# Two-layer hybrid encoder on one core: when the next layer's key and value weights are loaded, which engine copies the gates, and when gathered tokens are turned

## The chip, the cores and the metric

The kernel runs on one core of a Trainium2 chip. Its time is the device time of that core in microseconds (us), as the median of several executions. All arithmetic is in fp32 or in pairs of split values that together stand for fp32.

## The reference

A trunk of two layers on 512 tokens of 1024 features. Each layer has a mixing block, a cross-attention into 256 memory tokens, and 16 experts of which each picks its own 64 tokens. The change touches the third block and, inside it, the keys and values of the next layer's cross-attention.

```python
# cross-attention (one per layer): keys and values depend on mem and on weights alone
kv = (mem_n @ w_kv).reshape(b, m, 2, X_HEADS, X_HEAD_DIM)
...
# experts
logits = jnp.einsum('bsd,de->bse', h, w_router, preferred_element_type=jnp.float32)
aff = jax.nn.softmax(logits, axis=-1)
gates, idx = lax.top_k(aff.transpose(0, 2, 1), cap)
xs = h[b_ix, idx]
a = jnp.einsum('becd,edf->becf', xs, w_gate)
u = jnp.einsum('becd,edf->becf', xs, w_up)
y = jnp.einsum('becf,efd->becd', jax.nn.silu(a) * u, w_down)
y = y * gates[..., None].astype(y.dtype)
return jnp.zeros_like(h).at[b_ix, idx].add(y)
```

## The kernel before

**Pairs and steps.** The expert stage of a layer goes through eight pairs of experts (`pr` 0 to 7). A pair has 64 + 64 = 128 gathered tokens, one expert in each half of TensorE's columns. Its products come in eight chunks, after each of which `between(i)` runs what the tables `todo` and `plan` hold for that step: steps 0 to 3 follow four chunks of the gate and up products (32 matmuls of `xT`, two weight loads each), steps 4 to 7 four chunks of the down products (16 matmuls of `hT`, one load each). A pair therefore has twelve weight loads of 2 MB, which SyncE issues in order (`wload`, L1081).

**Weight buffers.** A load takes the next buffer of the list `order`, in rotation: seven of a ring ("w"), one in `kvp` ("k") and one in `pair` ("x"). A load waits until TensorE has read what stood in its buffer, and all later loads stand behind it in SyncE's queue. While the next layer's keys and values are computed, `kv_start` takes "k" and two of the ring out of the list, which leaves six; two come back after the last product.

**The tokens of the next pair** are found by VectorE and TensorE in steps 0 to 2, and fetched at step 3 (pair 0: step 4): GpSimd writes an iota, VectorE makes the indices, GpSimd starts an indirect transfer into the tile `xr` (`gather`, L1217). Each row of it carries 1024 features and the token's gates. `scalars` then copies three narrow columns (`rsl`, a token's scale, and `gx`, the gate of either expert) on GpSimd, behind the transfer. `next_turned` at steps 5 and 6 (pair 0: 6 and 7) turns the tokens into `xT` with 4 + 4 transposes on TensorE (L1203).

**What uses them.** ScalarE's `hs` (L1320) scales by `rsl`; `yhl` (L164 and L165, the split of a down result) scales by `gx`. `yhl` goes to TensorE, which scatters it back to the 512 tokens (L1339, L1340).

**Next layer's keys and values** are computed inside the expert stage of layer 0, at steps counted over all pairs (step 22 is pair 2, step 6). `kv_start` loads `mem` at 22 and takes the buffers, `mem_scaled` follows at 23, four `mem_turned` at 24 to 27 (L366 on TensorE). Then, eight times: `kv_load` brings 1 MB of weights at 28 + 4u, two `kv_split` at 29 + 4u and 30 + 4u make split copies of it on ScalarE and VectorE (L161, L162, tile `wkv`), `kv_products` at 31 + 4u multiplies. `mem` and all eight loads go through one buffer (tag "e") and GpSimd's queue, the queue of the gathers too (L1240). The place of an instruction in an engine's row is settled by a scheduler, which may move a transfer ahead of code written before it.

Of the kernel before, what the change touches and what calls it, by code (L numbers as in the profile page):

```python
# [29 lines left out]
D = 1024  # L30
# [5 lines left out]
NE = 16  # L36
# [55 lines left out]
def build(tc, a, out, packed):  # L92
    nc = tc.nc
# [4 lines left out]
    def pool(stack, name, bufs=1, **kw):  # L98
        return stack.enter_context(tc.tile_pool(name=name, bufs=bufs, reuse_waits="tile", **kw))
# [3 lines left out]
    pair = pool(es, "pair")  # L103
    RD, RM = 3, 7
    kvp = pool(es, "kvp", side="right")
    KV_STEP = 22
    ring, ex_ = [None], [None]
    order = deque()
    halves = []
# [10 lines left out]
    def bank2():  # L120
        turn[0] ^= 1
        return bank("ms"[turn[0]])
# [25 lines left out]
    def load(src, b, c):  # L148
        t = room(b, c)
        nc.sync.dma_start(t, src)  # L150
        return t
# [7 lines left out]
    def split_ps(p, hi, lo, col=None):  # L159
        if col is None:  # L160
            first = nc.scalar.activation(hi, p, AF.Copy)  # L161
            nc.vector.tensor_tensor(lo, p, hi.bitcast(F32), op=ALU.subtract)  # L162
        else:
            first = nc.scalar.activation(hi, p, AF.Copy, scale=col)  # L164
            nc.vector.scalar_tensor_tensor(lo, p, col, hi.bitcast(F32), op0=ALU.mult, op1=ALU.subtract)  # L165
        latest[0] = first
        return first
# [52 lines left out]
    def tsl(t):  # L220
        return slice(t * P, (t + 1) * P)

    def nosync(after, before, why):
        tc.add_manual_dep(after.ins, before.ins.name,
                          mybir.DependencyInfo(mybir.DependencyClass.NoSync, mybir.DependencyReason.DATA), reason=why)
# [32 lines left out]
    def col(base_, l, k):  # L258
        return cols[:, base_ + l * 8 + k:base_ + l * 8 + k + 1]
# [81 lines left out]
    def kv_tiles():  # L341

        if "k" in order:
            order.remove("k")
        t = kvp.tile([P, 2, 2048], F32, name="KV", tag="k")
        return shaped(t[:, 0], (KD, M)), shaped(t[:, 1], (2, D)), shaped(t[:, 0], (4, 512))
# [10 lines left out]
    def mem_scaled(mem, eng):  # L357
        for t in range(2):
            eng.tensor_scalar(mem[:, t], mem[:, t], rm[:, t:t + 1], None, op0=ALU.mult)

    def mem_turned(mem, mTs, k2):

        p = bank2()
        for i in range(2):
            for t in range(2):
                te(nc.tensor.transpose(p[:, tsl(i * 2 + t)], mem[:, t, tsl(2 * k2 + i)], ident))  # L366
        for i in range(2):
            k = 2 * k2 + i
            split_ps(p[:, i * M:(i + 1) * M], mTs[0][:, k], mTs[1][:, k], col(C_MEM, 0, k))
# [57 lines left out]
    for l in range(L):  # L427
# [240 lines left out]
        u = at.tile([P, TT, S], F32, name="u", tag="qd")  # L668
# [54 lines left out]
        if l == 0:  # L723
            mTs = [atp.tile([P, KD, M], F32R, name="mT", tag="a2") for _ in range(2)]
            mem = load(mem_src, 2, D)
# [220 lines left out]
        rows_d = rows_p.tile([S, W], F32, name=f"rows{l}")  # L946
# [168 lines left out]
        rsl = mp.tile([P, 8], F32, name="rsl")  # L1115
        gx = mp.tile([P, 8], F32, name="gx")
# [4 lines left out]
        def late():  # L1121

            if lp[0] is None:
                ey.close()
                lp[0] = pool(mo, f"late{l}")
            return lp[0]

        def scalars(pr, own, aff_at):

            nc.gpsimd.tensor_copy(rsl[:, pr:pr + 1], own[:, aff_at[2]:aff_at[2] + 1])  # L1130
            for e in range(2):
                sl = slice(e * 64, (e + 1) * 64)
                nc.gpsimd.tensor_copy(gx[sl, pr:pr + 1], own[sl, aff_at[e]:aff_at[e] + 1])

        def gather_first(oG, last):

# [62 lines left out]
        def turned(xT, k, xg):  # L1199

            p, n = bank2(), xg.shape[1] // P
            for i in range(n):
                te(nc.tensor.transpose(p[:, tsl(i)], xg[:, tsl(i)], ident))  # L1203
            g2 = cols[:, C_FFN + l * 8 + k:C_FFN + l * 8 + k + n]
            nc.vector.tensor_tensor(xT[:, k:k + n], p[:, 0:n * P].rearrange("p (i s) -> p i s", i=n),
                                    g2[:, :, None].broadcast_to([P, n, P]), op=ALU.mult)

        def gather(pr):

            xg = late().tile([P, W], F32, name="xr")  # L1210
            nc.gpsimd.iota(xg[:, 0:S], [[1, S]], base=0, channel_multiplier=0, allow_small_or_imprecise_dtypes=True)
            at = wk.tile([P, 1], F32, name="m", bufs=4)
            nc.vector.scalar_tensor_tensor(xg[:, S:2 * S], oSs[pr].bitcast(F32), 1.0, xg[:, 0:S], op0=ALU.mult,
                                           op1=ALU.mult, accum_out=at)
            idx = mp.tile([P, 1], I32, name="idx")
            nc.vector.tensor_copy(idx, at)
            nc.gpsimd.indirect_dma_start(xg, None, rows_d, bass.IndirectOffsetOnAxis(ap=idx, axis=0))  # L1217
            scalars(pr, xg, (D + 2 * pr, D + 2 * pr + 1, D + NE))
            return xg

        oG, last = rank_first()
# [9 lines left out]
        def planned(step, f, *args):  # L1231
            plan.setdefault(divmod(step, 8), []).append(functools.partial(f, *args))

        if l + 1 < L:
            kv = {}


            def kv_room(src, *dims):
                t = ex1.tile([P, *dims], F32, name="w", tag="e")
                nc.gpsimd.dma_start(t, src)  # L1240
                return t

            def kv_start():
                kv["out"] = kv_tiles()
                for nm in ("mT", "wkv"):
                    t = double([P, 2, KD, M], F32R, nm, True)
                    kv[nm] = t[:, 0], t[:, 1]
                kv["mem"] = kv_room(mem_src, 2, D)

            def kv_load(u):  # L1250
                kv["w"] = kv_room(piece(("xattn_w_kv", l + 1), 0, KD, u * M, M), KD, M)

            def kv_split(k0):
                for k in range(k0, k0 + 4, 2):
                    split_ps(kv["w"][:, k:k + 2], kv["wkv"][0][:, k:k + 2], kv["wkv"][1][:, k:k + 2])

            def kv_products(u):
                mh, ml = kv["mT"]
                ac = [bank("acc") for _ in range(2)]
                for k in range(KD):  # L1260
                    wh, wl = kv["wkv"][0][:, k], kv["wkv"][1][:, k]
                    for c in range(2):
                        if u < 4:
                            mm3(ac[c][:, 0:M], wh[:, tsl(c)], wl[:, tsl(c)], mh[:, k], ml[:, k], k == 0, k == KD - 1)
                        else:
                            mm3(ac[c][:, 0:M], mh[:, k, tsl(c)], ml[:, k, tsl(c)], wh, wl, k == 0, k == KD - 1)
                if u == 7:
                    order.extend("ww")
                for c in range(2):
                    dst = kv["out"][0][:, 2 * u + c] if u < 4 else kv["out"][1][:, c, (u - 4) * M:(u - 3) * M]  # L1270
                    nc.scalar.copy(dst, ac[c][:, 0:M])

            planned(KV_STEP, kv_start)
            planned(KV_STEP + 1, lambda: mem_scaled(kv["mem"], nc.gpsimd))
            for k2 in range(KD // 2):
                planned(KV_STEP + 2 + k2, lambda k2: mem_turned(kv["mem"], kv["mT"], k2), k2)
            for u in range(8):
                planned(KV_STEP + 6 + 4 * u, kv_load, u)
                planned(KV_STEP + 7 + 4 * u, kv_split, 0)
                planned(KV_STEP + 8 + 4 * u, kv_split, 4)  # L1280
                planned(KV_STEP + 9 + 4 * u, kv_products, u)
        carry = []

        def experts(pr, xT, hT_next, x_next):
# [3 lines left out]
            q = pr + 1  # L1288
            todo = [[] for _ in range(8)]
            rr, cc, xg, xT_next = [], {}, [], []  # L1290

            def later(i, f, *args):
                todo[i].append(functools.partial(f, *args))

            def next_turned(half):
                if not half:
                    xT_next.append(mp.tile([P, KD, P], F32, name="xT", tag="xT"))
                turned(xT_next[0], 4 * half, xg[0][:, 512 * half:512 * half + 512])

            todo[0] += carry  # L1300
            carry.clear()
            if q < NE // 2:
                todo[0].insert(min(1, len(todo[0])), lambda: rr.extend(rank_rows(q)))
                d = 1 if pr == 0 else 0
                for e in range(2):
                    later(e + d, lambda e: cc.update({e: rank_compare(q, e, rr)}), e)
                later(2 + d, lambda: rank_count(q, cc))
                later(3 + d, lambda: xg.append(gather(q)))
                for half in range(2):
                    later(5 + d + half, next_turned, half)  # L1310

            def between(i):
                for f in todo[i] + plan.get((pr, i), []):
# [184 lines left out]
```

## Time and profile before

| | before |
|---|---|
| median of 3 runs | 1671.43 us (1671.34 to 1671.88) |
| profiled execution | 1671.54 us, span 1669.7 us |
| PE busy | 1575.7 us, 94% of the span |
| DVE, ACT, POOL busy | 47%, 31%, 7% |
| HBM read | 474.14 MB, 288 GB/s over the span |
| chain that ended last | PE 77%, DMA 18%, DVE 2% |
| expert stage of layer 0 | about 394 to 886 us of the span |

PE is TensorE, DVE VectorE, ACT ScalarE, POOL GpSimd, SP SyncE. Shares of busy time are means over stages that have different limits, so the rows below look at stretches of the expert stage.

### The profile page before, as it was taken

The numbers are of one execution on the slowest core, as the hardware profiler recorded it, in microseconds if no ns is written. First come the engines' busy times: TensorE is split into PE (matmuls) and PEld (weight loads), VectorE is DVE, ScalarE is ACT, GpSimd is POOL, SyncE is SP. The second block draws the span as 40 slices with busy tenths as digits, with TensorE's granted clock in tenths as the row PEclk, the third lists the DMA queues.
The fourth block names the chain that finished last, engine by engine and source line by source line (L and its number), as shares of the span: only waits on it lengthen the run. The fifth ranks groups of instructions, "written<-read, shape, count | busy, mean of one in ns | idle before, by whom it ended". The sixth has DMA issues, their size and how long they took to land.

```text
span 1669.7 us, 20871 instructions
## 1 busy us (share of the span) xinstructions
PE 1575.7 (94%) x8154; PEld 923.9 (55%) x8154; DVE 781.7 (47%) x1836; ACT 513.4 (31%) x1057; POOL 110.4 (7%) x170
## 2 busy tenths in 40 slices
PE   9999999999799869999999999999999999888886
PEld 8667888874233324544548667888733333333333
DVE  5886646543243424334316886565434433342323
ACT  5676545441000111111115685454310000000002
POOL 1100000012200000000001100000210000000000
PEclk9999999999899979999999999999999999999998
DMA  6101332497899799999975102215899999999997
GB/s 215 73 26 52 125 127 101 195 381 306 360 425 427 315 426 414 426 426 427 426 322 177 54 26 76 77 50 241 344 372 427 427 426 426 427 428 426 426 428 288
DMA packets 48930, 481.86 MB, mean 289 GB/s; under 512 B 6592, under 2 KB 6976, under 8 KB 15552
## 3 DMA queue, kind: packets, MB, share of 16 engines
q1 hardware_dynamic: 42464, 459.03, 66.9%
q0 software_dynamic: 3440, 16.91, 2.5%
q10 hardware_dynamic: 2928, 4.59, 0.8%
q8 instruction: 64, 1.05, 0.3%
q14 instruction: 34, 0.28, 0.0%
HBM read 474.14 MB, written 6.37 MB: 288 GB/s over the span
## 4 chain that ended last, share of the span: by engine, by line
PE 77%; DMA 18%; DVE 2%; ACT 1%; issue 1%; POOL 0%; SPq 0%; DVEq 0%; ACTq 0%; POOLq 0%
PE acc L1352 29%; DMA w<-i_packed 16%; PE acc L170 10%; PE acc L171 10%; PE acc L172 10%; DMA xr<-rows,idx 2%; PE m L623 2%; PE m L613 2%; PE s L596 1%; PE acc L212 1%; PE s L597 1%; PE s L170 1%; PE s L171 1%; PE s L172 1%; PE s L1339 1%
## 5 line engine op out<-in xcount | busy, mean ns | idle before, releaser
L1352 PE MATMUL acc<-w,xT 128*64 128x512 f32 x2048 | 461.9, 596 | 24.7 <-DMA w<-i_packed 24.1
L1352 PEld LDWEIGHTS acc<-w,xT 128*64 128x64 f32 x2048 | 144.0, 137 | 307.1 <-issue 267.7
L1352 PE MATMUL acc<-w,hT 128*64 128x512 f32 (+1 forms) x1088 | 239.0, 583 | 38.8 <-DVE hT L1329 25.4
L1352 PEld LDWEIGHTS acc<-w,hT 128*64 128x64 f32 x1088 | 76.2, 139 | 167.0 <-issue 126.2
L164 ACT ACTIVATE yhl<-acc,gx 128x512 fp32r<-128x512 f32 (+1 forms) x34 | 22.5, 663 | 326.5 <-PE acc L1352 326.5
L1320 ACT ACTIVATE hs<-acc,rsl 128x512 f32<-128x512 f32 x32 | 22.0, 687 | 288.4 <-PE acc L1352 244.9
L162 DVE TENSOR_TENSOR wl<-w,wh 128x512 fp32r<-128x512 f32 x88 | 60.8, 694 | 85.7 <-ACT wh L161 83.3
L165 DVE SCALAR_TENSOR_TENSOR wl<-w,cols,wh 128x512 fp32r<-128x512 f32 (+1 forms) x96 | 68.9, 727 | 62.3 <-ACT wh L164 54.7
L161 ACT ACTIVATE wh<-w 128x512 fp32r<-128x512 f32 x88 | 55.2, 631 | 97.4 <-PE acc L172 81.0
L164 ACT ACTIVATE wh<-w,cols 128x512 fp32r<-128x512 f32 (+1 forms) x96 | 64.7, 687 | 63.0 <-PE acc L171 37.0
L170 PE MATMUL acc<-wh,a 128*128 128x512 f32 x192 | 77.8, 406 | 1.0 <-ACT wh L164 0.5
L1342 DVE TENSOR_TENSOR x<-m,x 128x512 f32<-128x512 f32 (+1 forms) x68 | 44.3, 651 | 72.9 <-PE m L1340 72.9
L171 PE MATMUL acc<-wl,a 128*128 128x512 f32 x192 | 76.8, 400 | 0.6 <-DVE wl L165 0.6
L172 PE MATMUL acc<-wh,a 128*128 128x512 f32 x192 | 77.0, 403 | 0.0
L1321 DVE SCALAR_TENSOR_TENSOR hs<-acc,rsl,hs 128x512 f32<-128x512 f32 x32 | 24.0, 749 | 112.1 <-PE acc L1352 111.8
L1342 DVE TENSOR_TENSOR x<-s,x 128x512 f32<-128x512 f32 (+1 forms) x68 | 44.3, 651 | 67.5 <-PE s L1340 67.5
L604 ACT ACTIVATE P<-s,nb,qsc 128x512 f32<-128x512 f32 x64 | 49.9, 781 | 10.1 <-DVE nb L601 9.5
L165 DVE SCALAR_TENSOR_TENSOR yhl<-acc,gx,yhl 128x512 fp32r<-128x512 f32 (+1 forms) x34 | 24.3, 715 | 58.2 <-ACT yhl L164 58.2
L170 PE MATMUL acc<-wh,o 128*128 128x512 f32 x128 | 51.5, 402 | 0.0
L1329 DVE COPY hT<-s 128x512 f32<-128x512 f32 x16 | 11.1, 692 | 86.4 <-PE s L1327 86.4
L172 PE MATMUL acc<-wh,o 128*128 128x512 f32 x128 | 50.0, 391 | 0.0
L171 PE MATMUL acc<-wl,o 128*128 128x512 f32 x128 | 50.0, 391 | 0.0
(426 smaller groups left out, 2934.9 us busy)
## 6 DMA issues: line engine op xcount, KB each, us to landing
w<-i_packed SPq DMA_DIRECT2D x166, 2048.0 KB, 19.7
w<-i_packed SPq DMA_DIRECT2D x84, 1024.0 KB, 8.2
w<-i_packed SPq DMA_DIRECT2D x24, 512.0 KB, 7.2
w<-i_packed POOLq DMA_DIRECT2D x8, 1024.0 KB, 11.9
rows<-x ACTq DMA_DIRECT2D x8, 512.0 KB, 5.1
x<-i_x SPq DMA_DIRECT2D x4, 512.0 KB, 5.9
KV<-i_packed SPq DMA_DIRECT2D x2, 1024.0 KB, 5.7
o_x<-o SPq DMA_DIRECT2D x4, 512.0 KB, 3.0
```

The lines of the kernel that those rows point to most:

```text
L161: first = nc.scalar.activation(hi, p, AF.Copy)
L162: nc.vector.tensor_tensor(lo, p, hi.bitcast(F32), op=ALU.subtract)
L164: first = nc.scalar.activation(hi, p, AF.Copy, scale=col)
L165: nc.vector.scalar_tensor_tensor(lo, p, col, hi.bitcast(F32), op0=ALU.mult, op1=ALU.subtract)
L170: te(nc.tensor.matmul(o, lh, rh, start=start, stop=False))
L171: te(nc.tensor.matmul(o, lh, rl, start=False, stop=False))
L172: te(nc.tensor.matmul(o, ll, rh, start=False, stop=stop))
L604: last_exp[0] = nc.scalar.activation(pt, s, AF.Exp, bias=nb, scale=qsc[:, t, h:h + 1], accum_out=rs)
L613: last_turn[0] = te(nc.tensor.transpose(p[:, tsl(t)], Ps[t][:, tsl(kt)], ident))
L623: now = te(nc.tensor.matmul(pv[i * 64:(i + 1) * 64], vv[:, kt, kvh * 64:(kvh + 1) * 64], PT[kt], start=kt == 0, stop=kt == TT - 1))
L1342: nc.vector.tensor_tensor(xs_, o, xs_, op=ALU.add)
L1352: te(nc.tensor.matmul(acc[e * 64:(e + 1) * 64], lhs(k)[:, e * 64:(e + 1) * 64], ws[e], start=k == 0, stop=k == KD - 1))
```

## The change

Four edits. `scalars` copies on ScalarE and is called at the start of the first turning, no longer straight behind the gather. The turnings move from steps 5 and 6 to 6 and 7 (pair 0: both at 7). The keys' and values' preparation starts at step 20 and not 22, but scaling and turning of `mem`, splits and products keep their steps; of the loads, the first goes from step 28 to 27, and each following one from 28 + 4u to 26 + 4u, the step in which the second split of the weights before it has freed the buffer. Last, the transfers of `mem` and of these weights are tied behind the latest gather in GpSimd's order (`nosync`: order alone, no wait).

```diff
-    KV_STEP = 22
+    KV_STEP = 20
...
-        def scalars(pr, own, aff_at):
-
-            nc.gpsimd.tensor_copy(rsl[:, pr:pr + 1], own[:, aff_at[2]:aff_at[2] + 1])
+        def scalars(pr, xg):
+
+            nc.scalar.copy(rsl[:, pr:pr + 1], xg[:, D + NE:D + NE + 1])
             for e in range(2):
                 sl = slice(e * 64, (e + 1) * 64)
-                nc.gpsimd.tensor_copy(gx[sl, pr:pr + 1], own[sl, aff_at[e]:aff_at[e] + 1])
+                nc.scalar.copy(gx[sl, pr:pr + 1], xg[sl, D + 2 * pr + e:D + 2 * pr + e + 1])
+
+        last_gather = [None]
...
-            nc.gpsimd.indirect_dma_start(xg, None, rows_d, bass.IndirectOffsetOnAxis(ap=idx, axis=0))
-            scalars(pr, xg, (D + 2 * pr, D + 2 * pr + 1, D + NE))
+            last_gather[0] = nc.gpsimd.indirect_dma_start(xg, None, rows_d, bass.IndirectOffsetOnAxis(ap=idx, axis=0))
...
-                nc.gpsimd.dma_start(t, src)
+                nosync(nc.gpsimd.dma_start(t, src), last_gather[0], "the tokens come first")
...
             planned(KV_STEP, kv_start)
-            planned(KV_STEP + 1, lambda: mem_scaled(kv["mem"], nc.gpsimd))
+            planned(KV_STEP + 3, lambda: mem_scaled(kv["mem"], nc.gpsimd))
             for k2 in range(KD // 2):
-                planned(KV_STEP + 2 + k2, lambda k2: mem_turned(kv["mem"], kv["mT"], k2), k2)
+                planned(KV_STEP + 4 + k2, lambda k2: mem_turned(kv["mem"], kv["mT"], k2), k2)
+            planned(KV_STEP + 7, kv_load, 0)
             for u in range(8):
-                planned(KV_STEP + 6 + 4 * u, kv_load, u)
-                planned(KV_STEP + 7 + 4 * u, kv_split, 0)
-                planned(KV_STEP + 8 + 4 * u, kv_split, 4)
-                planned(KV_STEP + 9 + 4 * u, kv_products, u)
+                planned(KV_STEP + 9 + 4 * u, kv_split, 0)
+                planned(KV_STEP + 10 + 4 * u, kv_split, 4)
+                if u < 7:
+                    planned(KV_STEP + 10 + 4 * u, kv_load, u + 1)
+                planned(KV_STEP + 11 + 4 * u, kv_products, u)
...
             def next_turned(half):
                 if not half:
                     xT_next.append(mp.tile([P, KD, P], F32, name="xT", tag="xT"))
+                    scalars(q, xg[0])
...
-                    later(5 + d + half, next_turned, half)
+                    later(min(6 + d + half, 7), next_turned, half)
```

GpSimd's row before, from the first gather of layer 0 (pair 0 fetches for pair 1) on; `xr<-rows_3748,idx` is a gather, `w<-i_mem` the transfer of `mem`, `w<-i_packed` one of the next layer's weights:

```order
27 L1240 DMA w<-i_mem 128x2x1024
28 L1217 DMA xr<-rows_3748,idx 128x1042
29 L359 TENSOR_SCALAR w<-w,rm 128x1024 x2
30 L1130 COPY rsl<-xr 128x1
31 L1133 COPY gx<-xr 64x1 x2
32 L1211 IOTA xr 128x512
33 L1217 DMA xr<-rows_3748,idx 128x1042
```

The same row after the change, from the first gather on:

```order
27 L1219 DMA xr<-rows_3748,idx 128x1042
28 L1213 IOTA xr 128x512
29 L1219 DMA xr<-rows_3748,idx 128x1042
30 L1213 IOTA xr 128x512
31 L1219 DMA xr<-rows_3748,idx 128x1042
32 L1241 DMA w<-i_mem 128x2x1024
33 L359 TENSOR_SCALAR w<-w,rm 128x1024 x2
34 L1213 IOTA xr 128x512
35 L1219 DMA xr<-rows_3748,idx 128x1042
36 L1241 DMA w<-i_packed 128x2048 x2
```

The transfer of `mem` has moved from ahead of the first gather to behind the third; the first weights come straight behind the fourth gather, with no copies between (before, they stand behind the copies of that gather).

ScalarE's row before, in pair 3 with the first weights' splits (`wkv`), and the `yhl` that ends the pair; `mT` are the split copies of the turned `mem`:

```order
304 L1320 ACTIVATE hs<-acc,rsl 128x512
305 L164 ACTIVATE mT<-s,cols 128x256 x2
306 L161 ACTIVATE wkv<-w 128x512 x4
307 L164 ACTIVATE yhl<-acc,gx 128x512 x2
308 L161 ACTIVATE wkv<-w 128x512 x3
```

The same place after:

```order
310 L1324 ACTIVATE hs<-acc,rsl 128x512
311 L1130 COPY rsl<-xr 128x1
312 L1133 COPY gx<-xr 64x1 x2
313 L164 ACTIVATE mT<-s,cols 128x256 x2
314 L161 ACTIVATE wkv<-w 128x512 x4
315 L164 ACTIVATE yhl<-acc,gx 128x512 x2
```

The three copies, which wait for the gather of the next pair, now stand ahead of the splits and of `yhl`. In pairs 0 to 2 they stand straight ahead of `yhl`.

SyncE's row in pair 2, at the place where three buffers leave the rotation, as a difference; the sixth load is the one that takes buffer "x", and the waits in brackets name the transfer that filled the buffer before (each load counts on the next of eight DMAHW counters, from the first row on):

```order
-L1081 DMA w<-i_packed 128x4096 [waits DMAHW3_49,PE_49]
-L1081 DMA w<-i_packed 128x4096 [waits DMAHW4_49,PE_49]
-L1081 DMA w<-i_packed 128x4096 [waits DMAHW5_49,PE_49]
-L1081 DMA w<-i_packed 128x4096 [waits DMAHW6_49]
-L1081 DMA w<-i_packed 128x4096 [waits DMAHW7_49,PE_49]
-L1081 DMA w<-i_packed 128x4096 [waits DMAHW5_49,DMAHW0_49,PE_49]
+L1081 DMA w<-i_packed 128x4096 [waits DMAHW5_49,DMAHW3_49,PE_49]
+L1081 DMA w<-i_packed 128x4096 [waits DMAHW4_49]
+L1081 DMA w<-i_packed 128x4096
+L1081 DMA w<-i_packed 128x4096 [waits DMAHW6_49,PE_49]
+L1081 DMA w<-i_packed 128x4096 [waits DMAHW7_49,PE_49]
+L1081 DMA w<-i_packed 128x4096 [waits DMAHW3_49,DMAHW0_49,PE_49]
```

Before, the sixth load takes the buffer that the third (DMAHW5) filled; now it takes that of the first (DMAHW3), and another of the six, the first, has moved into the place where a buffer is reused early.

## Rows read from the trace of the kernel before

**Rows 1.** Timeline of PE, pairs 0, 3 and 6: start, duration, what; [idle before <-releaser]

```profile
432.80 0.39 PE L1340 MATMUL m<-yhl,oS 128*128 128x512 f32 x1
...
443.96 1.09 PE L1203 MATMUL m<-ident,xr 128*128 128x128 f32 x4 [9.37 <-DMA xr<-rows,idx]
444.98 5.35 PE L1352 MATMUL acc<-w,hT 128*64 128x512 f32 x16
...
565.60 3.65 PE L1352 MATMUL acc<-w,xT 128*64 128x512 f32 x16 [2.50 <-DMA w<-i_packed]
571.82 5.08 PE L1352 MATMUL acc<-w,xT 128*64 128x512 f32 x16 [2.57 <-DMA w<-i_packed]
...
593.61 0.66 PE L366 MATMUL s<-ident,w 128*128 128x128 f32 x4
...
614.45 5.94 PE L1352 MATMUL acc<-w,hT 128*64 128x512 f32 x16 [16.02 <-DVE hT L1329]
...
849.13 7.09 PE L1352 MATMUL acc<-w,xT 128*64 128x512 f32 x32
```

**Rows 2.** Windows: start:end, length; PE, PEld, DVE, ACT, POOL busy; PEclk, DMA share, GB/s

```profile
440.00:460.00 20.00, 16.04 (x66) 6.47 (x67) 3.41 (x6) 0.69 (x1) 3.91 (x6) 0.79 0.74 289
540.00:560.00 20.00, 20.00 (x96) 7.65 (x93) 5.18 (x8) 1.38 (x2) 1.05 (x4) 1.00 0.50 194
620.00:860.00 240.00, 237.65 (x1278) 117.09 (x1277) 88.50 (x187) 35.92 (x64) 9.91 (x21) 1.00 1.00 423
1260.00:1640.00 380.00, 345.28 (x1619) 130.35 (x1618) 125.65 (x300) 25.01 (x39) 12.12 (x31) 1.00 1.01 426
```

**Rows 3.** Timeline of POOL around three gathers

```profile
420.10 0.96 POOL L1240 DMA_DIRECT2D w<-i_mem  x1 [1.40 <-PE acc L1352]
423.27 1.04 POOL L1217 DMA_INDIRECT xr<-rows,idx  x1 [2.21 <-DVE idx L1216]
...
588.88 0.96 POOL L1217 DMA_INDIRECT xr<-rows,idx  x1 [38.91 <-DVE idx L1216]
599.80 0.18 POOL L1130 COPY rsl<-xr 128x1 f32<-128x1 f32 x1 [9.96 <-DMA xr<-rows,idx]
...
600.28 0.58 POOL L1240 DMA_DIRECT2D w<-i_packed  x1
...
664.55 1.01 POOL L1217 DMA_INDIRECT xr<-rows,idx  x1 [25.81 <-DVE idx L1216]
```

**Rows 4.** All instructions of line L1217, the 14 gathers: issue to landing

```profile
DMA to landing us min/median/max: 10.9/11.2/20.6
```

**Rows 5.** Line L1240 from 560 to 830, the eight loads of key and value weights

```profile
DMA to landing us min/median/max: 5.9/11.9/13.0
```

**Rows 6.** Timeline of SP's queue, the weight loads around pair 2's end

```profile
502.08 7.19 SPq L1081 DMA_DIRECT2D w<-i_packed  x3
518.89 3.76 SPq L1081 DMA_DIRECT2D w<-i_packed  x3
552.90 7.19 SPq L1081 DMA_DIRECT2D w<-i_packed  x7
```

**Rows 7.** Line L1081, the load issued at 502.08

```profile
DMA to landing us min/median/max: 18.3/18.3/18.3
```

**Rows 8.** Line L1081, the load issued at 838.36

```profile
DMA to landing us min/median/max: 10.2/10.2/10.2
```

**Rows 9.** Line L251, a one-column copy on ACT: ns min/median/max

```profile
L251 ACT COPY m<-ones x1: 191/191/191, 2.9 to 2.9; 128x1 f32<-128x1 f32 x1
```

**Rows 10.** Timelines of ACT and DVE where weights are split, pairs 3 and 4

```profile
611.84 2.19 ACT L161 ACTIVATE wkv<-w 128x512 fp32r<-128x512 f32 x4 [16.04 <-DMA w<-i_packed]
...
612.50 1.29 DVE L162 TENSOR_TENSOR wkv<-w,wkv 128x512 fp32r<-128x512 f32 x2 [16.19 <-ACT wkv L161]
...
679.02 0.69 DVE L1329 COPY hT<-s 128x512 f32<-128x512 f32 x1 [2.90 <-PE s L1327]
```

**Rows 11.** The page's costliest groups, first halves of `yhl`: busy, mean ns

```profile
L164 ACT ACTIVATE yhl<-acc,gx 128x512 fp32r<-128x512 f32 (+1 forms) x34 | 22.5, 663 | 326.5 <-PE acc L1352 326.5
```

## The prediction

> **What bounds the kernel now.** I began with windows over the two expert stages, to see which engine is full in each [rows 2]. Layer 0, 620 to 860 us: PE is busy 237.65 of 240 us at a granted clock of 1.00, and the 16 DMA engines have a share of 1.00 at 423 GB/s. Both are full: whatever is to be gained there must give TensorE time and the transfers time as well. Layer 1, 1260 to 1640: the DMA share is 1.01 at 426 GB/s while PE has 345.28 of 380. The weights' transfer alone sets that stretch, and a change of when PE works moves its end by nothing. So the change is worth what it is worth in layer 0, before 620, where the windows have holes: 289 GB/s from 440 to 460, 194 GB/s from 540 to 560.
>
> Then PE's timeline there, for the idle time in brackets and what ended it [rows 1]. Three places matter. In pair 0 PE waits 9.37 us for the gathered tokens, and the 16 matmuls after it take 5.35 us where others take 3.65. At the start of pair 3 it waits 2.50 and 2.57 us for weights, the 16 matmuls after the second wait taking 5.08. At the end of that pair it waits 16.02 us for `hT`, and then 5.94 instead of 3.65. After each wait the matmuls are slow; in the window that holds the first wait the granted clock is 0.79 on average [rows 2], between the levels of 1.2 and 2.4 GHz. A removed wait thus gives back the slow chunk too.
>
> Each cause is on another queue. In pair 0 GpSimd issues `mem` at 420.10, 3.2 us ahead of the gather of 423.27 [rows 3]. That gather must be the one that lands after 20.6 us, the maximum of 14 with a median of 11.2 and a minimum of 10.9 [rows 4]: 423.27 + 20.6 = 443.9, and PE goes on at 443.96. In pair 3 the first key and value weights are issued at 600.28, behind the copies that waited 9.96 us for the gather of 588.88; ScalarE starts to split them at 611.84, VectorE stands in its second halves (612.50) [rows 10], and `hT` behind them. The weights of pair 3 are late because SyncE issues nothing from 522.7 to 552.90 [rows 6].
>
> **The change, term by term.** All in us, gains positive.
>
> *1. Pair 0, gather ahead of `mem`.* The wait and the slow chunk go: 9.37 + (5.35 - 3.65) = 11.1. A wait comes in: ScalarE's copies stand ahead of `yhl`. The gather of 423.27 lands at the median of 11.2 at 434.5. Three copies of 0.19 [rows 9], the first half of `yhl` in 0.66 [rows 11], the second on VectorE in about 0.65, half of the 1.29 for two such blocks [rows 10]: 436.4. PE's matmul with the second half ran at 432.80, so it comes 3.6 late. Behind that wait the next `hs` and the scatter stand, and no transfer. By then the tokens have landed, and both turnings stand together at step 7; the copy of the last into `xT` may be seen by PE for 0 to 0.7 (a 512-column copy is 0.69 [rows 10]); I take 0.2. Gain 11.1 - 3.6 - 0.2 = **7.3**; bounds 4.9 (a gather of 13.0 like the slowest other transfer of that queue [rows 5], and 0.7 seen) and 11.1.
>
> *2. Pair 3, the load in buffer "x".* The load at 552.90 waits for the last chunk of pair 2, since its buffer was filled only three loads before; now it is filled five loads before. It can go once PE has read pair 2's tenth load: earlier by two down chunks of 3.65 and what PE has between them, some 10, and by the 7.3 of term 1, so at about 535.5. That the buffer is an older one is read from the order, not the trace. A load took 18.3 where the queue was full [rows 7]: it lands at about 553.8, and PE wants it at 565.60 - 2.50 - 7.3 = 555.8. So 2.50 + 2.57 + (5.08 - 3.65) = **6.5** goes; bounds 0 and 6.5. But another load, the first of the new six, stands early too: as far as I can read the waits, SyncE stops there until PE is as far as it was at 518.89 [rows 6]. That costs transfer time (below), while five loads are still ahead of PE.
>
> *3. Pair 3, the first key and value weights.* They need not wait for the copies any more, but for their one buffer: the last transposes of `mem` run at 593.61 + 0.66 = 594.27, against an issue at 600.28, 6.0 earlier. But the gather of 588.88 is then still under way on the same queue. I take the landing at 13.0, the slowest of the eight, against 611.84 - 600.28 = 11.6 now: 6.0 - 1.4 = 4.6, and for a shorter wait some 0.3 less of slow chunk. **4.9**; bounds -3.4 (it is delayed by 9.4 as the gather was behind `mem`) and 11.7 (5.9, the fastest of the eight).
>
> *4. Pairs 4 to 6, copies ahead of the splits.* The gather issued at 664.55 lands at 675.8. Copies 0.6, four splits 2.2 [rows 10] and two key or value copies, which I put at 0.25 each: 679.0. VectorE's last second half 0.65 and then `hT` 0.69 end at 680.4, against 679.02 + 0.69 = 679.7 now. Three pairs lose 0.7 each: **-2.1**; bounds 0 (the scheduler's order leaves the pieces slack) and -4.
>
> *At nothing:* the copies themselves (24 of 0.19 on ScalarE, busy 35.92 of 240 where it is fullest [rows 2]); the turning a step later, hidden by a down chunk of 3.65, costing 0.7 a pair if that cover goes; the later loads u, issued two steps earlier, which are awaited nowhere now beyond the first; all of layer 1, since the transfers end it.
>
> Sum 7.3 + 6.5 + 4.9 - 2.1 = **16.6**. The profiled execution took 1671.54, so 1654.9; the median lies 0.1 lower. I predict 1655.0.
>
> **Can the transfers follow?** TensorE's gain counts only while weights arrive. What the two windows lose against 426 GB/s: (426 - 289)/426 x 20 = 6.4 and (426 - 194)/426 x 20 = 10.9, together 17.3. From it goes the new hole of term 2. SyncE's group of 502.08 comes some 7.3 earlier, lands its last bytes at about 510 to 512, and the next goes at 518.89 - 7.3 = 511.6, so after its start-up perhaps 3.4 are lost; bounds 0 and 10.9 (the old hole, only moved). Left: 13.9. To that comes the slack at the end of the stretch: the load issued at 838.36 lands after 10.2 [rows 8] at 848.56, and feeds the second half of the group at 849.13 + 7.09/2 = 852.7 [rows 1], 4.1 later. So the transfers allow 18.0, more than 16.6, but not much more.
>
> The Trainium skill, "DMA: Bandwidth & Descriptors", section "Issuing engines are not separate DMA queues", speaks against the change: whoever starts a transfer, it runs on the same 16 DMA engines and interleaves with the rest, so earlier key and value weights only take their bytes from the experts' weights. The share of 1.00 at 423 GB/s agrees. By that rule alone the gain would be the recovered 13.9, and the time 1657.6; I take TensorE's sum because of the slack of 4.1.
>
> **The rivals.**
>
> *A. Transfers land sooner (0.11).* The gather in 10.9, the first key and value weights in 5.9, both the minima [rows 4, 5]: 0.3 and 6.8 more, 23.7. For it: nothing but the gather stands ahead on that queue. Against: the median of the eight is 11.9. The transfers' 18.0 cap it: 1653.5. For 1 MB the Trainium skill, "DMA: Bandwidth & Descriptors", section "Anatomy of one DMA — SWDGE (gpsimd) path", would give an estimate of 2.0 + 1048576/436000 = 4.4 us; no run here shows less than 5.9.
>
> *B. The hole only moves (0.13).* SyncE's new early reuse costs as much as the old one, 10.9. Then the transfers allow 17.3 - 10.9 + 4.1 = 10.5, and term 2 is lost: 1661.0. For it: six buffers in rotation, one of them reused out of turn, in both orders. Against: it comes while five loads are ahead.
>
> *C. The first key and value weights wait behind the gather (0.09)* as the gather did behind `mem`: term 3 is -3.4, the sum 8.3, the time 1663.2. For it: the one pair of such neighbours that the trace shows [rows 3, 4]. Against: the gather is then 5.4 ahead, not 3.2 behind.
>
> *D. No change to be told (0.08).* B and C together: 7.3 + 0 - 3.4 - 2.1 = 1.8, 1669.7. Of this kernel, 0.2% (3.3 us) is about what a measurement can tell from no change, and it is within that.
>
> *E. Slower (0.07): the copies hold `yhl` in every pair.* They stand ahead of it on ScalarE wherever tokens are fetched. In pairs 1 to 6 of layer 0 the gather is issued a step earlier than in pair 0, so it has what pair 0 has until `yhl` (432.80 - 423.27 less 2.0 for copies and halves, 7.5) and a gate or up chunk of 7.09 more: 14.6. A gather that lands by then delays nothing. At 20.6 each of six pairs would lose 6.0, 36.0 in all, for a gain of 16.6: 1690.9. It decides from a landing of about 14.6 + 16.6/6 = 17.4. For it: transfers are now packed tighter. Against: half of the 14 gathers land within 0.3 of the minimum [rows 4].
>
> **How the numbers follow.** Forecast 0.52, A 0.11, B 0.13, C 0.09, D 0.08, E 0.07. Faster: forecast, A, B and C, 0.85; same D, 0.08; slower E, 0.07. D and E, 0.15, are left out of the range. It goes from 1649, at which the transfers' allowance without any new hole (17.3 + 4.1 = 21.4, 1650) is just inside, to C's 1663.2 and a little more: 1649 to 1664.
>
> **What would show it.** Right: the first gather near 11 us, no wait of 9 at the transposes of pair 0 but one of 3 to 4 at its scatter; no weight waits at the start of pair 3; the wait for `hT` in pair 3 at 11 to 12 instead of 16; waits of `hT` in pairs 4 to 6 a little longer. The GB/s of 540 to 560 near 426, with a small hole near 510. Layer 1 as long as before. Wrong: a stop of SyncE that empties the transfers somewhere else; `w` among PE's releasers in layer 0 after 620; gathers above 15 us; `yhl` waited for in each pair.

## The result and the profile after

The changed kernel took 1660.89 us (median of four, 1659.54 to 1662.09), the kernel before 1671.63 on the same chip: a ratio of 0.9936, 95% interval 0.9918 to 0.9953, so 10.7 us faster. The forecast was 1655.0 with a range of 1649 to 1664. The profiled execution is the slowest of the four (1662.09, span 1660.3).

Three of the prediction's four terms come out within 1.4 us, the first is 2.8 us too large, and a place that it had set to nothing gives 4.6 us back. I read it off the start of the same matmul in both traces: counting the matmuls of the experts' products (line L1352 before, L1356 after), and taking off the small difference that the two executions have at the stage's first one, the changed kernel leads by:

| at the start of | before, us | lead, us | the term's gain | forecast |
|---|---|---|---|---|
| pair 1 of layer 0 (193rd product) | 450.8 | 4.5 | 4.5 | 7.3 |
| pair 3, third gate/up chunk (641st) | 577.4 | 11.4 | 6.9 | 6.5 |
| pair 3, third down chunk (737th) | 620.9 | 16.5 | 5.1 | 4.9 |
| pair 7, last down chunk of layer 0 (1537th) | 878.3 | 13.0 | -3.5 | -2.1 |
| pair 1 of layer 1, last gate/up chunk (1857th) | 1289.6 | 8.4 | -4.6 | 0 |
| last product (3136th) | 1655.0 | 9.4 | 1.0 | 0 |

The first row of the table rests on PE's timeline around pair 0's scatter; with it stand the waits for `hT` in pairs 3, 4 and 5, and the scatter in pair 0 of layer 1:

```profile
436.24 0.80 PE L1343 MATMUL m<-yhl,oS 128*128 128x512 f32 x1 [3.54 <-ACT yhl L164]
...
439.76 0.63 PE L1344 MATMUL s<-yhl,oS 128*128 128x512 f32 x1
440.31 4.84 PE L1356 MATMUL acc<-w,hT 128*64 128x512 f32 x16
...
446.53 7.09 PE L1356 MATMUL acc<-w,xT 128*64 128x512 f32 x32 [0.35 <-DVE xT L1207]
...
599.13 9.08 PE L1356 MATMUL acc<-w,hT 128*64 128x512 f32 x32 [11.92 <-DVE hT L1333]
...
664.58 7.09 PE L1356 MATMUL acc<-w,hT 128*64 128x512 f32 x32 [1.56 <-DVE hT L1333]
...
728.46 8.78 PE L1356 MATMUL acc<-w,hT 128*64 128x512 f32 x32 [2.00 <-DVE hT L1333]
...
1246.88 0.50 PE L1343 MATMUL s<-yhl,oS 128*128 128x512 f32 x1 [2.80 <-ACT yhl L164]
...
1250.42 4.27 PE L1356 MATMUL acc<-w,hT 128*64 128x512 f32 x16
```

The wait of 9.37 us for the tokens [rows 1] is gone, and one of 3.54 us for `yhl` stands in its place, as forecast (3.6). What the forecast left out is behind it: eight scatter matmuls take 4.07 us (436.24 to 440.31), where they take some 2.1 without the wait, and the next chunk 4.84 instead of 3.65. The wait for `hT` in pair 3 fell from 16.02 to 11.92; the two waits for weights at its start are gone.

ScalarE's timeline shows who holds `yhl`: the copies wait for the gather, and `yhl` stands behind them.

```profile
435.00 0.19 ACT L1130 COPY rsl<-xr 128x1 f32<-128x1 f32 x1 [15.98 <-DMA xr<-rows,idx]
435.09 0.39 ACT L1133 COPY gx<-xr 64x1 f32<-64x1 f32 x2
435.50 0.69 ACT L164 ACTIVATE yhl<-acc,gx 128x512 fp32r<-128x512 f32 x1
```

On GpSimd's timeline the gather of pair 0 goes first, and the first weights (583.35) go without a copy ahead of them:

```profile
423.45 1.17 POOL L1219 DMA_INDIRECT xr<-rows,idx  x1 [4.58 <-DVE idx L1218]
...
577.68 1.07 POOL L1219 DMA_INDIRECT xr<-rows,idx  x1 [21.88 <-DVE idx L1218]
583.35 0.57 POOL L1241 DMA_DIRECT2D w<-i_packed  x1 [4.60 <-PE s L366]
```

Issue to landing, of all 14 gathers (line L1219), where the slowest no longer takes 20.6 [rows 4]:

```profile
DMA to landing us min/median/max: 10.9/11.2/12.1
```

The same of the load of 583.35 (line L1241), for which 13.0 was assumed:

```profile
DMA to landing us min/median/max: 13.2/13.2/13.2
```

The windows (columns as in [rows 2]) show the transfers. From 440 to 460 the stop of TensorE leaves a hole: 347 GB/s. From 540 to 560 they are full, 429 GB/s instead of 194; the new stop of the weight queue costs (429 - 316)/429 x 10 = 2.6 us at 510 to 520 (3.4 was taken). But in layer 1, 1250 to 1280, they fall to 386, where the kernel before (the last line) has 425.

```profile
440.00:460.00 20.00, 19.65 (x91) 7.99 (x92) 8.59 (x22) 1.77 (x3) 0.56 (x1) 0.93 0.87 347
510.00:520.00 10.00, 10.00 (x50) 3.40 (x48) 5.98 (x21) 0.69 (x1) 0.00 (x0) 1.00 0.84 316
540.00:560.00 20.00, 20.00 (x100) 9.25 (x98) 8.45 (x17) 2.13 (x4) 6.20 (x3) 1.00 1.01 429
620.00:860.00 240.00, 234.39 (x1256) 113.85 (x1255) 82.18 (x179) 34.36 (x71) 7.40 (x11) 0.99 0.99 418
1250.00:1280.00 30.00, 29.65 (x139) 11.26 (x138) 13.75 (x38) 2.46 (x4) 0.56 (x1) 0.97 0.97 386
1250.00:1280.00 30.00, 29.60 (x140) 12.15 (x142) 13.43 (x34) 3.13 (x5) 1.05 (x4) 1.00 1.01 425
```

SP's queue says why: in pair 0 of layer 1 it issues nothing between 1244.45 and 1254.74, because the buffer it wants is read by the chunk of 1250.42, which stands behind the scatter that waits for `yhl`. SP's longest wait for TensorE there is 10.2 us; it is 7.3 in gp_pair0, where that scatter does not wait for the copies. In layer 0, from 430 to 460, it is 12.1 against 6.1.

```profile
1240.69 3.76 SPq L1081 DMA_DIRECT2D w<-i_packed  x2
...
1254.74 0.33 SPq L1081 DMA_DIRECT2D w<-i_packed  x1
```

**The theory** from this: ScalarE's copies, waiting for the gather ahead of `yhl`, cost twice. In layer 0 they stop TensorE for 3.5 us, and the matmuls behind take 3 more than they would; in layer 1 that stop holds a weight buffer and leaves a hole in transfers that bound the stage. **Rival 1**: the later turning of the tokens, both halves at step 7, does it. **Rival 2**: transfers cap layer 0 anyway, so nothing would be gained there without the stop.

### The profile page after: what moved, and what is told of

Same layout as the page of the kernel before. It is cut to its first block, busy times and chain, and to the rows that moved or that the text cites. A ratio compares the mean times of both kernels' runs of the same rounds, so it can differ in the third digit from the quotient of the medians.

```text
span 1660.3 us, 20836 instructions
## 1 busy us (share of the span) xinstructions
PE 1578.6 (95%) x8154; PEld 925.0 (56%) x8154; DVE 781.4 (47%) x1836; ACT 518.5 (31%) x1099; POOL 102.2 (6%) x128
## 5 line engine op out<-in xcount | busy, mean ns | idle before, releaser
L1356 PE MATMUL acc<-w,xT 128*64 128x512 f32 x2048 | 460.7, 595 | 19.6 <-DMA w<-i_packed 18.3
L1356 PEld LDWEIGHTS acc<-w,xT 128*64 128x64 f32 x2048 | 142.6, 137 | 297.7 <-issue 257.3
L1356 PE MATMUL acc<-w,hT 128*64 128x512 f32 (+1 forms) x1088 | 240.4, 589 | 34.6 <-DVE hT L1333 25.4
L1356 PEld LDWEIGHTS acc<-w,hT 128*64 128x64 f32 x1088 | 77.4, 141 | 172.2 <-issue 132.6
L165 DVE SCALAR_TENSOR_TENSOR yhl<-acc,gx,yhl 128x512 fp32r<-128x512 f32 (+1 forms) x34 | 24.3, 716 | 89.6 <-ACT yhl L164 89.6
L1333 DVE COPY hT<-s 128x512 f32<-128x512 f32 x16 | 11.1, 691 | 82.4 <-PE s L1331 82.4
## 6 DMA issues: line engine op xcount, KB each, us to landing
w<-i_packed SPq DMA_DIRECT2D x166, 2048.0 KB, 21.9
```

Source lines behind the costliest of these rows:

```text
L1356: te(nc.tensor.matmul(acc[e * 64:(e + 1) * 64], lhs(k)[:, e * 64:(e + 1) * 64], ws[e], start=k == 0, stop=k == KD - 1))
```

## The experiments

The leads over the kernel before, as in the table above, of the profiled execution of each. Every ratio is to the kernel before on the same chip; its medians on these chips lie between 1670.5 and 1671.6, so times of different chips compare to about 1 us:

| kernel | time, us | ratio, 95% interval | pair 1 | 641st | 737th | end of layer 0 | layer 1, pair 1 |
|---|---|---|---|---|---|---|---|
| changed | 1660.89 | 0.9936 [0.9918, 0.9953] | 4.5 | 11.4 | 16.5 | 13.0 | 8.4 |
| gp_pair0 | 1650.04 | 0.9877 [0.9861, 0.9894] | 11.3 | 18.2 | 24.3 | 21.2 | 21.6 |
| gp_pair0_again | 1650.87 | 0.9880 [0.9864, 0.9897] | 11.3 | 18.2 | 23.8 | 20.3 | 20.8 |
| turn_early | 1660.97 | 0.9938 [0.9921, 0.9954] | 4.9 | 11.8 | 16.0 | 12.1 | 8.0 |
| gp_layer0 | 1655.15 | 0.9913 [0.9896, 0.9930] | 11.3 | 18.2 | 24.3 | 21.0 | 15.8 |
| mem_behind | 1689.04 | 1.0107 [1.0091, 1.0124] | 11.6 | 12.5 | 11.2 | -18.8 | -18.3 |
| mem_only_order | 1659.60 | 0.9934 [0.9917, 0.9950] | 11.1 | 12.4 | 12.4 | 12.4 | 13.2 |
| kv_early | 1663.75 | 0.9957 [0.9943, 0.9971] | 0.0 | 6.9 | 6.5 | 6.5 | 7.2 |
| copies_gpsimd | 1652.10 | 0.9890 [0.9873, 0.9906] | 11.3 | 18.2 | 18.4 | 19.1 | 19.4 |
| mem_fast | 1649.73 | 0.9878 [0.9862, 0.9894] | 11.3 | 17.3 | 27.4 | 21.6 | 21.9 |
| fast_gpsimd | 1649.32 | 0.9874 [0.9857, 0.9890] | 11.3 | 17.2 | 32.7 | 20.9 | 21.3 |

**gp_pair0: the copies of pair 0 off ScalarE.**

```diff
+            copy = nc.gpsimd.tensor_copy if pr == 1 else nc.scalar.copy
-            nc.scalar.copy(rsl[:, pr:pr + 1], xg[:, D + NE:D + NE + 1])
+            copy(rsl[:, pr:pr + 1], xg[:, D + NE:D + NE + 1])
...
-                nc.scalar.copy(gx[sl, pr:pr + 1], xg[sl, D + 2 * pr + e:D + 2 * pr + e + 1])
+                copy(gx[sl, pr:pr + 1], xg[sl, D + 2 * pr + e:D + 2 * pr + e + 1])
```

> The changed kernel, but the copies for the tokens fetched in pair 0 stand on GpSimd again, so that they no longer hold yhl on ScalarE; all else as changed. The theory (the copies' wait is the loss): TensorE's wait of 3.5 us at the scatter of pair 0 goes in both layers, and the slow matmuls behind it too, about 6.7 us in layer 0 (TensorE is then 11 and not 4.3 us ahead of before at pair 1), and in layer 1 the hole in the transfers, about 4 us: 1650 to 1653. Rival 1 (it is the later turning that costs, both at step 7): as the changed kernel, 1660 to 1662. Rival 2 (the transfers cap the gain of layer 0): TensorE gains the 6.7 at pair 1 and loses most of it to waits for weights before the end of layer 0, only layer 1 keeps its 4: about 1657.

1650.04 us, 10.9 below the changed kernel (and below turn_early, which ran on the same chip). Its PE timeline in pair 0:

```profile
434.81 3.65 PE L1357 MATMUL acc<-w,hT 128*64 128x512 f32 x16
...
439.84 7.09 PE L1357 MATMUL acc<-w,xT 128*64 128x512 f32 x32 [0.35 <-DVE xT L1208]
```

Its windows, where the changed kernel had its holes:

```profile
440.00:460.00 20.00, 20.00 (x96) 7.90 (x96) 11.78 (x35) 1.77 (x3) 0.19 (x1) 1.00 1.01 427
1250.00:1280.00 30.00, 29.36 (x146) 11.43 (x144) 14.38 (x40) 2.45 (x4) 0.97 (x1) 1.00 1.01 427
```

The chunk after the scatter takes 3.65 again, pair 1 starts 6.7 us sooner, and both holes in the transfers are filled. Of 6.7, 3.54 is the wait, 4.84 - 3.65 = 1.2 the chunk, and the rest, 2.0, the scatter at the lower clock. Layer 0 keeps the gain to its end (21.2), and TensorE waits for no weights in it, so rival 2 fails here; layer 1 loses none. Run a second time beside fast_gpsimd, the same kernel took 1650.87.

> gp_pair0 once more, on the same chip as fast_gpsimd, so that the two can be compared: 1650 by either theory.

**turn_early: the turning back at its old steps.**

```diff
-                    later(min(6 + d + half, 7), next_turned, half)
+                    later(5 + d + half, next_turned, half)
```

> The changed kernel with the tokens turned at steps 5 and 6 again (pair 0: 6 and 7). The theory (the copies' wait): the copies stand ahead of yhl all the same, so the scatter of pair 0 still waits some 3.5 us and the time stays at 1660 to 1662. Rival 1 (the later turning costs): the slow stretch of pair 0 in both layers goes and the time is about 1654.

1660.97 us, no difference from the changed kernel; the scatter waits as long (PE's timeline):

```profile
436.32 0.80 PE L1343 MATMUL m<-yhl,oS 128*128 128x512 f32 x1 [3.62 <-ACT yhl L164]
```

Rival 1 falls: turning later neither costs nor gains anything in the time (the 0.35 us that PE waits for `xT` at 446.53 above is all that shows of it in pair 0).

**gp_layer0: the stop left in layer 1 alone.** As gp_pair0, with `if pr == 1 and l == 0`.

> As gp_pair0, but the copies of pair 0 stand on GpSimd in layer 0 alone; in layer 1 they hold yhl on ScalarE as in the changed kernel. The theory (in layer 1 the stop of TensorE holds weight buffers, so the transfers that bound that stage run dry): layer 0 as in gp_pair0, TensorE 21 us ahead of before at its end, and 4 to 5 us lost again in pair 0 of layer 1: 1654 to 1655. Rival (layer 1 ends with its transfers whatever TensorE does, as the prediction had it): 1650, as gp_pair0.

1655.15 us, 5.1 above gp_pair0 (4.8 when each is taken against the kernel before on its own chip). Up to the end of layer 0 the two have the same leads, and then 5.2 us are lost in pair 0 of layer 1, as its PE timeline shows:

```profile
1239.03 0.80 PE L1344 MATMUL s<-yhl,oS 128*128 128x512 f32 x1 [3.75 <-ACT yhl L164]
```

The transfers there, by the window:

```profile
1250.00:1280.00 30.00, 30.00 (x148) 11.46 (x146) 13.03 (x38) 2.45 (x4) 0.96 (x1) 1.00 0.98 402
```

The lowest rate is 342, from 1240 to 1250. The landings of SyncE's weight loads show that the transfers themselves come later: in pair 0 of layer 1 those of both kernels are some 21.5 us ahead of the kernel before; by the end of the layer those of gp_pair0 are 21.8 ahead, those of gp_layer0 17.0. A stage that is bound by its transfers is not safe from a stop of TensorE.

**mem_behind: the order behind the gathers alone**, put on the kernel before.

```diff
-                nc.gpsimd.dma_start(t, src)
+                nosync(nc.gpsimd.dma_start(t, src), last_gather[0], "the tokens come first")
```

> The kernel before with one edit: mem and the key and value weights are tied behind the latest gather. The theory: the gather of pair 0 lands in about 11 us, the wait of 9.4 us and its slow chunk go (11.1), no new wait comes; the waits of pair 3 stay (2.5, 2.6 and 16.0 us), and so does the stop of the weight queue; layer 1 stays as it was. The transfers give back 6.4 and have a slack of 4.1, so 1671.6 - 10.5, about 1661. Rival 2 (the transfers cap it lower, since the stop of the queue empties them as long as before): TensorE's gain is lost again to waits for weights before 886, 1665 or more.

1689.04 us: slower by 18, where I expected 1661. The first half came out as expected (a lead of 11.6 at pair 1), and I had missed what the order does later. GpSimd's timeline, with the second load, the gather of pair 4 and the third load:

```profile
603.31 0.54 POOL L1242 DMA_DIRECT2D w<-i_packed  x1 [15.25 <-DVE wkv L162]
...
652.37 1.02 POOL L1219 DMA_INDIRECT xr<-rows,idx  x1 [36.79 <-DVE idx L1218]
653.38 0.55 POOL L1242 DMA_DIRECT2D w<-i_packed  x1
```

PE's timeline in pairs 4 and 5:

```profile
674.99 5.64 PE L1354 MATMUL acc<-w,hT 128*64 128x512 f32 x16 [8.18 <-DVE hT L1331]
...
748.09 6.63 PE L1354 MATMUL acc<-w,hT 128*64 128x512 f32 x16 [8.89 <-DVE hT L1331]
```

The third load is written at step 36, just after the gather of step 35. Without the order the scheduler lets it go when its buffer is free; with it, it waits for the gather's place. It lands too late for its splits, VectorE stands in them, and `hT` behind: 8.18 + 5.64 - 3.65 = 10.2 us, and by the leads 9 to 11 in each of pairs 4 to 6.

**mem_only_order: the same for `mem` alone.**

```diff
+                now = nc.gpsimd.dma_start(t, src)
+                if src is mem_src:
+                    nosync(now, last_gather[0], "the tokens come first")
```

> As mem_behind, but only mem is tied behind the latest gather; the key and value weights stand where the scheduler put them before. Theory 1 (in mem_behind the third, fifth and seventh of these loads were held behind the gathers of pairs 4 to 6, about 29 us): that loss goes, TensorE keeps the 12.7 us of pair 0, capped by the transfers at 10.5: 1658 to 1661. Rival (mem itself lands too late or takes the weights' time): as mem_behind, 1685 or more.

1659.60 us. The third load goes ahead of the gather again, and none of the 12.4 us is lost later (GpSimd's timeline):

```profile
626.57 0.54 POOL L1242 DMA_DIRECT2D w<-i_packed  x1 [10.44 <-DVE wkv L162]
...
652.92 1.01 POOL L1219 DMA_INDIRECT xr<-rows,idx  x1 [25.81 <-DVE idx L1218]
```

So the order for `mem` alone, 11.3 us, gives what the whole change gives. In the changed kernel the order does no such harm: the loads are written two steps earlier, the third at step 34, and it goes at 622.23, ahead of the gather of 648.58. So the order on the key and value weights needs the new steps; the new steps do not need the order, as the next run shows. The changed kernel without the order was not run.

**kv_early: the new steps alone**, put on the kernel before (`KV_STEP = 20` and the five `planned` lines of the change).

> The kernel before with one edit: the new steps of the key and value work (buffers taken at step 20, loads earlier), with no order behind the gathers. The theory: only the weight load of pair 3 gains, 2.5 + 2.6 and the slow chunk, 6.5, since the first key and value weights still stand behind GpSimd's copies: about 1665. A rival (the new hole in the transfers takes it back): TensorE waits for weights at the end of layer 0, 1669 to 1671.

1663.75 us: 6.8 us gained by the median, 6.9 at the 641st product, and next to nothing taken back. The stop has moved to 500 to 520 and is shorter, by the windows:

```profile
500.00:520.00 20.00, 20.00 (x98) 7.85 (x94) 11.35 (x34) 2.45 (x4) 0.00 (x0) 1.00 0.93 382
540.00:560.00 20.00, 20.00 (x95) 7.87 (x92) 5.18 (x8) 1.37 (x2) 1.04 (x4) 1.00 1.00 424
```

The wait for `hT` in pair 3 stays (PE's timeline):

```profile
607.71 6.01 PE L1354 MATMUL acc<-w,hT 128*64 128x512 f32 x16 [16.37 <-DVE hT L1331]
```

**copies_gpsimd: all copies on GpSimd.** Both `nc.scalar.copy` of `scalars` are `nc.gpsimd.tensor_copy`, still called at the turning.

> The changed kernel with all copies of rsl and gx on GpSimd, at the turning. The theory: pair 0 gains in both layers as in gp_pair0; the first key and value weights stand behind the copies of pair 3 again and come some 5 us later, so the wait for hT there is 16 to 17 and not 11.5 us; pairs 4 to 6 win back the 2.6 us that the changed kernel lost there. If the transfers cap layer 0 all the same: 1650; if not: about 1653. Rival (the copies on ScalarE are worth more than their wait): 1655 or more.

1652.10 us. The first weights stand behind the copies again (581.85, straight after them), the lead does not rise between the 641st and the 737th product (18.2 to 18.4, where gp_pair0 rises by 6.1), and nothing is lost in pairs 4 to 6 (where gp_pair0 loses 3.1). GpSimd's timeline:

```profile
581.37 0.18 POOL L1130 COPY rsl<-xr 128x1 f32<-128x1 f32 x1 [9.81 <-DMA xr<-rows,idx]
581.50 0.41 POOL L1133 COPY gx<-xr 64x1 f32<-64x1 f32 x2
581.85 0.57 POOL L1241 DMA_DIRECT2D w<-i_packed  x1
```

PE's timeline, with the wait for `hT`:

```profile
596.09 9.79 PE L1356 MATMUL acc<-w,hT 128*64 128x512 f32 x32 [16.07 <-DVE hT L1333]
```

So terms 3 and 4 both hang on where the copies of pairs 1 to 6 stand; the places in the trace tell them apart. PE waits for no weights in layer 0 here, so the transfers do not cap this kernel, and 1652.10 lies nearer to the 1653 expected for that.

**mem_fast: gp_pair0 with the first weights well ahead.**

```diff
-                planned(KV_STEP + 4 + k2, lambda k2: mem_turned(kv["mem"], kv["mT"], k2), k2)
-            planned(KV_STEP + 7, kv_load, 0)
+                planned(KV_STEP + 4 + k2 // 2, lambda k2: mem_turned(kv["mem"], kv["mT"], k2), k2)
+            planned(KV_STEP + 5, kv_load, 0)
```

> As gp_pair0, with the turning of mem squeezed from four steps into two (24 and 25) and the first key and value weights loaded at step 25, so that they land well before their splits; all else the same. TensorE's wait of 11.5 us for hT in pair 3 and 1.5 us of slow matmuls should go. Theory 1 (the transfers are full from 430 us on and cap layer 0): what TensorE gains there it loses again to waits for weights before the end of layer 0: 1647 to 1650. Theory 2 (TensorE is the bound, the transfers follow): 1637 to 1639.

1649.73 us, the same as gp_pair0. The wait of 11.5 us has become one of 5.56 (ScalarE's copies, waiting for the gather, now stand in front of splits whose weights are there), and what else was gained is gone again by the end of layer 0 (27.4 to 21.6), 4.7 us of it in five waits for weights. So here the transfers do decide; the next kernel takes the last wait away too.

**fast_gpsimd: mem_fast with all copies on GpSimd.**

> mem_fast with every copy of rsl and gx on GpSimd, so that neither the splits of pairs 3 to 6 nor yhl stand behind the gather on ScalarE; the first key and value weights are issued ahead of the gather of pair 3 and so stand behind no copy. TensorE's wait of 5.6 us in pair 3 of mem_fast goes and the 2.7 us of pairs 4 to 6 too. Theory 1 (transfers full at 425 GB/s from 430 to 840 cap layer 0): waits for weights take their place, and the time stays within 1.5 us of gp_pair0 and mem_fast: 1648 to 1650. Theory 2 (TensorE is the bound): 8 us below mem_fast, about 1641.

1649.32 us, the lowest median, but only 1.5 us below gp_pair0 on the same chip (1650.87), and their intervals overlap. TensorE's lead rises to 32.7 us at the 737th product and falls to 20.9 at the end of layer 0. PE's waits from 420 to 840 (total, times, longest):

```profile
PE acc L1356 <- DMA w<-i_packed: 14.9, 12, 1.7
PE acc L1356 <- DVE hT L1333: 4.7, 6, 0.8
```

Ten of the twelve waits for weights come behind the start of the 737th product and take 11.8 us, which is what the lead falls by. Its window of that stretch:

```profile
430.00:840.00 410.00, 390.71 (x2017) 177.95 (x2014) 152.43 (x343) 52.19 (x93) 24.68 (x44) 1.00 1.01 425
```

The same window of the kernel before has 407 GB/s:

```profile
430.00:840.00 410.00, 375.55 (x1902) 168.08 (x1900) 151.35 (x340) 51.91 (x92) 23.25 (x43) 0.96 0.97 407
```

(425 - 407)/425 x 410 = 17.4 us of transfer time was all that could be recovered there, and with the slack of some 4 us at the end of the stage (4.1 by the prediction) that is the 21 us at which mem_fast and fast_gpsimd end layer 0. gp_pair0 ends it at 21.2 too, its transfers at 425 GB/s over the same window, but without a wait for weights: its own gains happen to add up to the cap.

## Why the prediction was near and where it failed

The sum of 16.6 came out 7.2 too high in the profiled execution: term 1 was 2.8 too large, term 4 1.4 and layer 1, which was put at nothing, took 3.6, while terms 2 and 3 were 0.6 too small.

- **Term 1, pair 0 (7.3 forecast, 4.5 measured): mis-sized.** The mechanism and the new wait were right (3.6 forecast, 3.54 measured; the gather landed after 11.5). For the removed wait the slow chunk behind it was counted, for the added one it was not: the 3.2 us of slow scatter and chunk that gp_pair0 gives back are most of the error. With it the term would have been 11.1 - 3.6 - 3.2 - 0.2 = 4.1.
- **Term 2, weights of pair 3 (6.5; 6.9 here and in kv_early): right**, with the new stop of the queue costing 2.6 of transfers where 3.4 was taken. Rival B did not come.
- **Term 3, first weights (4.9; 5.1): right.** Issue to landing was 13.2 where 13.0 was taken; rivals A and C did not come. copies_gpsimd puts the term back to 0.2.
- **Term 4, pairs 4 to 6 (-2.1; -3.5 here, -3.1 in gp_pair0): right in kind, some 1 us too small, and not three times the same.** The waits for `hT` are 1.56, 2.00 and 1.26 where the kernel before has 0.78 each, 2.5 us more in all, near the forecast. But behind the 2.00 of pair 5 the 32 matmuls take 8.78 instead of 7.09, which the forecast left out, and 2.2 of the 3.5 are lost there. copies_gpsimd takes the term away.
- **"all of layer 1, since the transfers end it", put at nothing: this step failed.** It was 4.6 us at pair 1, of which 1.0 comes back later; by gp_layer0 some 5 us in the time. Transfers bound that stage, but a load goes only once TensorE has read its buffer, so "a change of when PE works moves its end by nothing" does not hold for a stop that lasts. I looked at the wait behind `yhl` for what stood there and wrote "no transfer"; in both layers the chunk behind that scatter releases one.
- **The turning a step later, put at nothing: right** (turn_early). **Rival E**, a loss in every pair, did not come: the slowest gather took 12.1 us, against the 14.6 at which it starts.
- **The cap by the transfers** (18.0 forecast) did not bind in the changed kernel, which ends layer 0 at 13.0 and waits nowhere for weights there, nor in gp_pair0. The allowance itself was too large: the 6.4 us to be recovered from 440 to 460 came back only in part, since the new stop leaves (427 - 347)/427 x 20 = 3.7 of them lost. The cap binds in mem_fast and fast_gpsimd, at about 21. There, earlier key and value weights move no more bytes per microsecond (425 GB/s from 430 to 840 in gp_pair0 and in fast_gpsimd), and what fast_gpsimd loses of its lead of 32.7 us goes in waits for the experts' weights. The Trainium skill, "DMA: Bandwidth & Descriptors", section "Issuing engines are not separate DMA queues", says that transfers run on the same 16 DMA engines and interleave with each other, whichever engine starts them; these runs agree, with 425 GB/s in both.

What stays open: why the wait of 2.00 us in pair 5 was followed by slow matmuls and that of 1.56 in pair 4 was not. The four executions of the changed kernel spread over 2.6 us where those of the kernel before, on that chip, spread over 0.5; on the other chips those of the kernel before spread over 3.5 to 5.0 themselves, so this says nothing of the change.

## What to carry to other kernels

A small instruction that waits for a transfer stops everything behind it on its engine, so put it on the engine with nothing urgent behind it at that place, and count for a new wait on TensorE the slow matmuls that may follow it, as for a removed one. A transfer-bound stage still needs buffers released in time: ask of each stall which load its next chunk lets go. And an ordering edge put on a shared helper binds all its callers; here it was worth 11 us for one of them and cost some 30 us on the others until those were written earlier.

## What the hardware did that I had not expected

One wait of 3.54 us in an otherwise full stretch was followed by slow matmuls. In the changed kernel the granted clock is 0.50, the level of 1.2 GHz, over the scatter (436.24 to 440.31), 0.75 on average over the chunk behind it, and 1.00, the level of 2.4 GHz, from 444 to 460; in gp_pair0, which does not wait there, it is 1.00 from 430 to 460. The chunk of 16 takes 4.84 us against 3.65, and the stop costs 6.7 us for 3.54 of waiting.

The length of a single wait did not tell what followed. In pair 5 of the changed kernel 2.00 us were followed by a granted clock of 0.50 from 730 to 732; in the kernel before, the 2.50 us at 565.60 [rows 1] left the chunk behind it at 3.65, so the prediction's "After each wait the matmuls are slow" goes too far. In fast_gpsimd twelve waits for weights of up to 1.7 us, 14.9 in all, leave the granted clock of 430 to 840 at 1.00.
